# Residual, carried norms and scaled copies: one block per slot, and no POOL weight block in the attention output and the first feed-forward quad

## The chip, the cores and the metric

One NeuronCore of a Trainium2 chip runs the whole program. The metric is the time of one execution on the device in microseconds, lower is better. Engines have short names here: PE (TensorE, matmul), PEld (its weight loads), DVE (VectorE), ACT (ScalarE), POOL (GpSimd), SP (SyncE, which issues the DMAs). Each engine works through its own instructions in a fixed order; an instruction that waits holds up those behind it on the same engine.

## The reference

A decoder layer for 256 prompt tokens and 8 sample tokens, D_MODEL 2048, in fp32:

```python
def decoder_layer(x, mem_k, mem_v, st, p):
    y, st_new = token_mixers(x, st, p)          # four branches, gated, merged, @ w_out
    x = layer_norm(DN_ALPHA * x + y, p["ln1_g"], p["ln1_b"])
    x = layer_norm(DN_ALPHA * x + memory_attention(x, mem_k, mem_v, p), p["ln2_g"], p["ln2_b"])
    x = layer_norm(DN_ALPHA * x + sq_relu_mlp(x, p), p["ln3_g"], p["ln3_b"])
    return x, st_new

def layer_norm(x, g, b):
    mu = jnp.mean(x, axis=-1, keepdims=True)
    var = jnp.mean(jnp.square(x - mu), axis=-1, keepdims=True)
    return (x - mu) * lax.rsqrt(var + LN_EPS) * g + b

def memory_attention(x, mem_k, mem_v, p):       # 4 heads of 128, 256 memory tokens
    q = x @ p["xq_w"]
    a = softmax(q . mem_k * XDH ** -0.5)
    return (a . mem_v) @ p["xo_w"]

def sq_relu_mlp(x, p):                          # 2048 -> 8192 -> 2048
    h = jnp.square(jax.nn.relu(x @ p["ffn_w1"] + p["ffn_b1"]))
    return h @ p["ffn_w2"] + p["ffn_b2"]
```

The token mixers (a delta rule, two convolutions, an mLSTM) come first and take the first half of the time; the change does not touch them.

## The kernel before

**Layout.** Activations are kept transposed: 128 features by 264 tokens is one block, and a row of 2048 features is 16 blocks (`KB`). `y` holds the residual stream, one block per `d`.

**Precision.** Every large product is made of three matmuls in fp32r: an operand is split into a high part (rounded) and a low part (the rest), and high × high, high × low and low × high are summed in PSUM. For weights, `wh` and `wl` are made on the chip: ACT rounds `raw` into `wh` (`feed`), and DVE or POOL subtracts to get `wl` (`feed_lo`). For activations the pairs are `xh`/`xl`, `zh`/`zl`, `hgh`/`hgl`, `mh`/`ml`.

**Slots.** The program is one long list of slots. A slot is a weight block of 128 × 1024 and its 24 matmuls. While slot s runs on PE, `run` (L287) issues `wh` and `wl` of slot s + 2 and the load of slot s + 5 (`dma_w`; three `raw` buffers). Every `every[0]`-th block has its `wl` made on POOL (`slot`, L206): every fourth at first, every third from the query projection on (L1448), every second from the first feed-forward layer on (L1667).

**Work between slots.** Work that no slot owns is written as Python generators, which `run` steps once or more a slot: `chain` (one step when DVE is not behind by its own estimate `dv_t`) and `fill` (as many steps as that estimate leaves room for). What is issued then goes through a scheduler, which orders the instructions of each engine by a simulated timeline; `after(i, "DVE")` ties an instruction behind the last `wl` of DVE, and nothing else holds a generator's work to the slot in which it was issued. The generators that matter here:
- `residual` (L1307) writes ALPHA·x, less a rough mean `m`, into `y` from the pair `xh`, `xl`, during the last branch's projection.
- `Norm` (L377) gathers the sums of y and y² block by block (`add`: the squares on ACT, the even blocks' sums on POOL, the odd ones' on DVE) and makes mean and 1/σ from them (`finish`).
- `carry` (L1361) rewrites `y` for the next residual: (y − mean)·(ALPHA·g)·(1/σ) + ALPHA·b for 16 blocks, with every second subtraction on POOL (`Norm.block`) and the shift `ab` on ACT.

**The norm inside a product.** The product after a norm does not wait for the norm. It multiplies by y·g (`z_block`, L1331: `zh` on ACT, `zl` on DVE), with two more columns for the sums over g and b (`zpair`), and the mean and 1/σ are put in when PSUM is read (`z_post`, L1337).

**Stages around the change**, in slots: the last branch's projection with its gates (`stage2`, L1373); output projection `wout`, 32; query projection, 8, in a quad (four PSUM banks at once); memory keys, 8; memory values, 8, with the attention (`attn`) as a chain beside both; attention output `xo`, 8 (L1626, two banks `gxo` a slot); the first quad of the first feed-forward layer, 8; the rest of the hidden group (24 slots); then output and hidden groups by turns, to the final norm. PE has four PSUM banks for products (`pg`, L95).

## Time and profile before

| | |
|---|---|
| median of 3 runs | 2326.68 us (2324.32 to 2328.25) |
| the profiled execution | 2324.7 us, span 2322.9 us |
| PE busy | 2249.0 us, 97% of the span |
| DVE, ACT, POOL busy | 1269.8, 1167.0, 977.8 us |
| mean granted clock of PE | 0.990 |

A busy time is a sum over the whole span. Where PE is idle, and at which clock it runs after it, is read from windows of some stages; 1.00 there is the higher of two levels of the clock, 2.4 GHz, and 0.50 the lower one, 1.2 GHz. A duration in the trace overlaps with that of the next instruction on the same engine; what an instruction costs in a queue is the distance between two starts.

### The profile page before, as it was taken

Reading aid. Unit: us, or ns where it says so; the run is one execution under the profiler, and the core shown is the slowest. Engines: PE = TensorE matmul, PEld = TensorE weight load, DVE = VectorE, ACT = ScalarE, POOL = GpSimd, SP = SyncE. Lnnn points to the kernel's source line nnn. Section 1 sums busy time; section 2 is a strip of 40 time slices with the busy share of each in tenths; the row PEclk is TensorE's granted clock in tenths of the full one; section 3 lists DMA queues with packets and bytes.
Section 4 is the critical chain, followed back from the end, with each engine's and each line's share of the span. In section 5 each row is a group of like instructions: output and inputs, shape, how many; then the busy total and the mean of one; then the engine's idle time right before and its main releaser. Section 6 shows DMA issues by size and latency. Waiting matters only on the chain.

```text
span 2322.9 us, 46442 instructions
## 1 busy us (share of the span) xinstructions
PE 2249.0 (97%) x19034; PEld 2205.4 (95%) x19034; DVE 1269.8 (55%) x2039; ACT 1167.0 (50%) x1789; POOL 977.8 (42%) x733
## 2 busy tenths in 40 slices
PE   9899999989999999999989999989999999999997
PEld 8899898989999999999989998889999999999997
DVE  7998998894464455433474566385323323323323
ACT  6756456554554455544434555456435435534543
POOL 4535335341222133433243365165445544544576
PEclk9999999999999999999999999999999999999998
DMA  7556455554656676765556666545565565566553
GB/s 233 166 151 201 137 174 167 169 165 143 193 173 185 195 221 215 211 182 182 182 183 182 200 200 201 187 132 181 181 182 176 179 182 181 174 183 181 176 180 127
DMA packets 125134, 418.81 MB, mean 180 GB/s; under 512 B 15608, under 2 KB 20984, under 8 KB 124920
## 3 DMA queue, kind: packets, MB, share of 16 engines
q1 hardware_dynamic: 124920, 415.84, 58.4%
q8 instruction: 149, 2.44, 0.4%
q14 instruction: 65, 0.53, 0.1%
HBM read 401.37 MB, written 14.41 MB: 179 GB/s over the span
## 4 chain that ended last, share of the span: by engine, by line
PE 81%; DVE 13%; issue 3%; DMA 1%; ACT 1%; POOL 1%; DVEq 0%; POOLq 0%; ACTq 0%; SPq 0%
PE g L150 73%; DVE cB L139 3%; DVE wl L128 3%; PE q L150 1%; DVE cu L139 1%; DVE y L128 1%; PE pv L150 1%; DVE y L139 1%; DMA dbc<-dd 1%; PE ub L150 0%; PE xb L150 0%; DVE s L139 0%; PE cb L150 0%; ACT wh L123 0%; PE nb L150 0%
## 5 line engine op out<-in xcount | busy, mean ns | idle before, releaser
L123 ACT ACTIVATE wh<-raw 128x1024 fp32r<-128x1024 f32 (+1 forms) x705 | 745.4, 1058 | 822.4 <-PE g L150 306.3
L128 POOL TENSOR_TENSOR wl<-raw,wh 128x1024 fp32r<-128x1024 f32 x240 | 588.0, 2450 | 724.7 <-PE g L150 483.2
L150 PE MATMUL g<-xh,wl 128*128 128x264 f32 x2496 | 714.0, 286 | 8.1 <-DVE wl L128 6.0
L150 PE MATMUL g<-xl,wh 128*128 128x264 f32 x2496 | 717.2, 287 | 0.0
L150 PE MATMUL g<-xh,wh 128*128 128x264 f32 x2496 | 716.1, 287 | 0.9 <-ACT wh L123 0.9
L128 DVE TENSOR_TENSOR wl<-raw,wh 128x1024 fp32r<-128x1024 f32 (+1 forms) x465 | 589.8, 1269 | 231.2 <-PE g L150 169.6
L150 PEld LDWEIGHTS g<-xh,wl 128*128 128x128 f32 x2496 | 473.0, 190 | 10.2 <-DVE wl L128 6.6
L150 PEld LDWEIGHTS g<-xh,wh 128*128 128x128 f32 x2496 | 473.5, 190 | 5.3 <-issue 2.5
L150 PEld LDWEIGHTS g<-xl,wh 128*128 128x128 f32 x2496 | 472.2, 189 | 2.3 <-issue 1.3
L150 PE MATMUL g<-hgh,wl 128*128 128x264 f32 x1024 | 290.4, 284 | 0.0
L150 PE MATMUL g<-hgl,wh 128*128 128x264 f32 x1024 | 290.4, 284 | 0.0
L150 PE MATMUL g<-hgh,wh 128*128 128x264 f32 x1024 | 289.9, 284 | 0.0
L150 PE MATMUL g<-zh,wh 128*128 128x266 f32 x960 | 275.1, 287 | 0.8 <-DVE zw L128 0.8
L150 PE MATMUL g<-zl,wh 128*128 128x266 f32 x960 | 274.6, 286 | 0.0
L150 PE MATMUL g<-zh,wl 128*128 128x266 f32 x960 | 274.4, 286 | 0.0
L150 PEld LDWEIGHTS g<-hgl,wh 128*128 128x128 f32 x1024 | 193.0, 188 | 0.0
L150 PEld LDWEIGHTS g<-hgh,wh 128*128 128x128 f32 x1024 | 192.5, 188 | 0.0
L150 PEld LDWEIGHTS g<-hgh,wl 128*128 128x128 f32 x1024 | 192.4, 188 | 0.0
L128 DVE TENSOR_TENSOR y<-y,g 128x264 f32<-128x264 f32 x80 | 34.3, 429 | 278.7 <-PE g L150 278.7
L150 PEld LDWEIGHTS g<-zh,wh 128*128 128x128 f32 x960 | 181.4, 189 | 1.0 <-ACT wh L123 1.0
L150 PEld LDWEIGHTS g<-zl,wh 128*128 128x128 f32 x960 | 181.7, 189 | 0.0
L150 PEld LDWEIGHTS g<-zh,wl 128*128 128x128 f32 x960 | 180.8, 188 | 0.0
(481 smaller groups left out, 3449.3 us busy)
## 6 DMA issues: line engine op xcount, KB each, us to landing
raw<-in_win_dram SPq DMA_DIRECT2D x312, 512.0 KB, 4.0
raw<-in_f_dram SPq DMA_DIRECT2D x248, 512.0 KB, 4.2
raw<-in_wbr_dram SPq DMA_DIRECT2D x64, 512.0 KB, 4.0
raw<-in_wout_dram SPq DMA_DIRECT2D x32, 512.0 KB, 4.3
s<-in_sS_dram SPq DMA_DIRECT2D x8, 512.0 KB, 5.0
dbc<-dd SPq DMA_DIRECT2D x16, 256.0 KB, 3.7
out_S_s_dram<-s SPq DMA_DIRECT2D x8, 512.0 KB, 5.2
c<-in_sCm_dram SPq DMA_DIRECT2D x8, 512.0 KB, 5.7
```

Of the source, the lines that this page charges most:

```text
L123: return AC.activation(out, in_, func, bias=bias, scale=scale, **kw)
L128: return (eng or DV).tensor_tensor(out=out, in0=a, in1=b, op=op)
L139: return DV.scalar_tensor_tensor(out=out, in0=a, scalar=s, in1=b, op0=op0, op1=op1)
L150: PE.matmul(out, lhsT, rhs, start=start, stop=stop)
```

## The change

Five edits.
- A third queue, `pace`: `run` steps it exactly once a slot, before the others and without a look at the estimate. The residual, both `carry` generators and the new `z_two` go through it.
- In `residual` each block is two instructions on DVE (the subtraction of `m` goes into the first of them, and none is on POOL), tied behind the last `wl`, with a `yield` after each block.
- In `carry` both instructions of a block run on DVE and are tied behind the last `wl`; ACT's addition of the shift is gone, and the shift is added with the attention output and with the first output group of the feed-forward layer, in one instruction with the addition of the product.
- `z_block` scales on ACT into a buffer `zf`, rounds that on ACT into `zh`, and subtracts on DVE. After the attention output it no longer stands in the slot's `post` but in `z_two`, one block a slot until all products are there and two a slot then, tied behind the last `wl`; the carried norm follows in the same generator.
- `every[0] = 0` from the attention output on: no `wl` on POOL there and in the first quad of the feed-forward layer, until `every[0] = 2`.

```diff
     def slot(src, fn, post=None):
         seen[0] += 1
-        on_pool = len(slots) > 8 and seen[0] % every[0] == 0
+        on_pool = len(slots) > 8 and every[0] and seen[0] % every[0] == 0
...
                 feed_lo(s + 2)
+            if pace:
+                step(pace)
             if chain and dv_t[0] < lim:
...
-        def block(self, d, gcol, pool=False):
+        def block(self, d, gcol, pool=False, held=False):
             t = self.y[:, d, :]
-            tt(t, t, self.mu, SUB, eng=GP if pool else None)
-            stt(t, t, gcol, self.rs, MUL, MUL)
+            x = tt(t, t, self.mu, SUB, eng=GP if pool else None)
+            y = stt(t, t, gcol, self.rs, MUL, MUL)
+            if held:
+                after(x, "DVE")
+                after(y, "DVE")
...
         for d in range(KB):
             t = y[:, d, :]
-            ts(t, al[:, d, :].bitcast(F32), ALPHA, MUL)
-            if d:
-                tt(t, t, m[:], SUB, eng=GP if d % 2 else None)
-            stt(t, ah[:, d, :].bitcast(F32), ALPHA, t, MUL, ADD)
+            if d == 0:
+                after(ts(t, al[:, d, :].bitcast(F32), ALPHA, MUL), "DVE")
+            else:
+                after(stt(t, al[:, d, :].bitcast(F32), ALPHA, m[:], MUL, SUB), "DVE")
+            after(stt(t, ah[:, d, :].bitcast(F32), ALPHA, t, MUL, ADD), "DVE")
+            yield
...
-    def z_block(n, d):
+    def z_block(n, d, held=False):
         zh, zl = yt["z" + n]
         g, y = col(yt["zg"], d), yt["y"][:, d, :]
-        act(zh[:, d, 0:NT], y, AF.Copy, scale=g)
-        stt(zl[:, d, 0:NT], y, g, zh[:, d, 0:NT].bitcast(F32), MUL, SUB)
+        z = tp.tile([P, 30 + NT], F32, tag="extB", name="zf")[:, 0:NT]
+        act(z, y, AF.Copy, scale=g)
+        act(zh[:, d, 0:NT], z, AF.Copy)
+        x = tt(zl[:, d, 0:NT], z, zh[:, d, 0:NT].bitcast(F32), SUB)
+        if held:
+            after(x, "DVE")
...
         for d in range(KB):
-            t = ln.block(d, yt["ag"][:, i, d:d + 1], pool=d % 2)
-            act(t, t, AF.Identity, bias=yt["ab"][:, i, d:d + 1])
-            if d % 2:
-                yield
+            ln.block(d, yt["ag"][:, i, d:d + 1], held=True)
+            yield
...
+    def z_two(ln):
+        for d in range(KB):
+            while yt["ny"] <= d:
+                yield
+            z_block("2", d, held=True)
+            ln.add(d)
+            if yt["ny"] < KB or d % 2 or d == KB - 1:
+                yield
+        yield from carry(1, ln)
...
     mark(xo_start)
+    every[0] = 0
...
                 t = yt["y"][:, d, :]
-                tt(t, t, yt["pxo"][i], ADD)
-                z_block("2", d)
-                yt["ln"].add(d)
+                stt(t, yt["pxo"][i], yt["ab"][:, 0, d:d + 1], t, ADD, ADD)
+            yt["ny"] += 2
...
-                tt(t, t, ps, ADD)
+                if g:
+                    tt(t, t, ps, ADD)
+                else:
+                    stt(t, ps, yt["ab"][:, 1, d:d + 1], t, ADD, ADD)
```

How the instructions of DVE stand before and after, at three places. A row names the line, the operation, what it writes and reads, the shape and, where it repeats, how often.

The residual on DVE, before (`y<-xl` and `y<-xh,y` make a block, `m` is the rough mean, `wl` a weight block's low part, `gate` and `ml` the branch's own work):

```order
L133 TENSOR_SCALAR y<-xl 128x264 x11
L133 TENSOR_SCALAR gb<-pc 128x16
L143 COPY gb<-pc 128x16
L128 TENSOR_TENSOR wl<-raw,wh 128x1024
L128 TENSOR_TENSOR ab<-ab,bm 128x32
L128 TENSOR_TENSOR y<-y,m_14309 128x264 x8
L128 TENSOR_TENSOR gate<-g,gate 128x264
L139 SCALAR_TENSOR_TENSOR y<-xh,y 128x264
L128 TENSOR_TENSOR wl<-raw,wh 128x1024
L139 SCALAR_TENSOR_TENSOR y<-xh,y 128x264 x12
L128 TENSOR_TENSOR wl<-raw,wh 128x1024
```

The same place after:

```order
L128 TENSOR_TENSOR wl<-raw,wh 128x1024
L128 TENSOR_TENSOR ab<-ab,bm 128x32
L128 TENSOR_TENSOR y<-y,m_14340 128x264
L138 SCALAR_TENSOR_TENSOR y<-xl,m_14340 128x264
L138 SCALAR_TENSOR_TENSOR y<-xh,y 128x264
L128 TENSOR_TENSOR gate<-g,gate 128x264
L128 TENSOR_TENSOR wl<-raw,wh 128x1024
L138 SCALAR_TENSOR_TENSOR y<-xl,m_14340 128x264
L128 TENSOR_TENSOR ml<-merged,mh 128x264
L138 SCALAR_TENSOR_TENSOR y<-xh,y 128x264
L128 TENSOR_TENSOR wl<-raw,wh 128x1024
```

Twelve blocks stood between two `wl`; now one block does, or two where a block of POOL falls between.

The first carried norm on DVE at the query projection, before (`a` holds the norm's sums, then mean and 1/σ; `q_...` are the quad's banks):

```order
L128 TENSOR_TENSOR y<-y,a_15921 128x264 x5
L139 SCALAR_TENSOR_TENSOR a_15921<-q,a_15920 128x264
L128 TENSOR_TENSOR y<-y,a_15921 128x264 x3
L128 TENSOR_TENSOR wl<-raw,wh 128x1024
L139 SCALAR_TENSOR_TENSOR y<-y,ag,a_15921 128x264 x12
L128 TENSOR_TENSOR wl<-raw,wh 128x1024
L139 SCALAR_TENSOR_TENSOR y<-y,ag,a_15921 128x264 x4
L128 TENSOR_TENSOR wl<-raw,wh 128x1024 x2
L143 COPY zw<-q_17056 128x2
```

The same place after:

```order
L138 SCALAR_TENSOR_TENSOR a_15906<-q,a_15905 128x264
L128 TENSOR_TENSOR wl<-raw,wh 128x1024
L128 TENSOR_TENSOR y<-y,a_15906 128x264
L138 SCALAR_TENSOR_TENSOR y<-y,ag,a_15906 128x264
L128 TENSOR_TENSOR wl<-raw,wh 128x1024
L128 TENSOR_TENSOR y<-y,a_15906 128x264 x2
L138 SCALAR_TENSOR_TENSOR y<-y,ag,a_15906 128x264 x2
L128 TENSOR_TENSOR wl<-raw,wh 128x1024
L128 TENSOR_TENSOR y<-y,a_15906 128x264
L138 SCALAR_TENSOR_TENSOR y<-y,ag,a_15906 128x264
L128 TENSOR_TENSOR wl<-raw,wh 128x1024
```

The pieces of 8, 12 and 4 have become blocks of one or two between the `wl`; POOL's eight subtractions are among them.

The attention output on DVE, before, from the third product on (`gxo` is a product, `zl` the low scaled copy, `a` the odd blocks' norm sums):

```order
L128 TENSOR_TENSOR y<-y,gxo 128x264
L128 TENSOR_TENSOR wl<-raw,wh 128x1024
L139 SCALAR_TENSOR_TENSOR zl_18158<-y,pc,zh_18157 128x264
L128 TENSOR_TENSOR a_18156<-a_18156,ln_z 128x264
L128 TENSOR_TENSOR a_18156<-a_18156,y 128x264
L139 SCALAR_TENSOR_TENSOR zl_18158<-y,pc,zh_18157 128x264
L128 TENSOR_TENSOR y<-y,gxo 128x264 x2
L139 SCALAR_TENSOR_TENSOR zl_18158<-y,pc,zh_18157 128x264
L128 TENSOR_TENSOR a_18156<-a_18156,ln_z 128x264
L128 TENSOR_TENSOR a_18156<-a_18156,y 128x264
L128 TENSOR_TENSOR y<-y,gxo 128x264 x2
L128 TENSOR_TENSOR wl<-raw,wh 128x1024
```

The same place after:

```order
L138 SCALAR_TENSOR_TENSOR y<-gxo,ab,y 128x264
L128 TENSOR_TENSOR wl<-raw,wh 128x1024
L128 TENSOR_TENSOR zl_18159<-zf,zh_18158 128x264
L128 TENSOR_TENSOR a_18157<-a_18157,ln_z 128x264
L128 TENSOR_TENSOR a_18157<-a_18157,y 128x264
L138 SCALAR_TENSOR_TENSOR y<-gxo,ab,y 128x264 x2
L128 TENSOR_TENSOR zl_18159<-zf,zh_18158 128x264
L128 TENSOR_TENSOR wl<-raw,wh 128x1024
L128 TENSOR_TENSOR a_18157<-a_18157,ln_z 128x264
L128 TENSOR_TENSOR zl_18159<-zf,zh_18158 128x264
L128 TENSOR_TENSOR a_18157<-a_18157,y 128x264
L138 SCALAR_TENSOR_TENSOR y<-gxo,ab,y 128x264 x2
```

One `zl` a slot stands there in place of two, and a `wl` in every slot; the norm's sums are not tied and stand as they did.

On SP's queue the four loads of `cv` for the second half of the samples stand one block earlier, ahead of the fourth block of the memory values' weights instead of behind it.

## Rows read from the trace of the kernel before

**Rows 1.** The page, its first line and part 1 (busy, share, instructions).

```profile
span 2322.9 us, 46442 instructions
PE 2249.0 (97%) x19034; PEld 2205.4 (95%) x19034; DVE 1269.8 (55%) x2039; ACT 1167.0 (50%) x1789; POOL 977.8 (42%) x733
```

**Rows 2.** Waits of PE, 1100 to 1700 us: total, times, longest.

```profile
PE q L150 <- DVE wl L128: 8.1, 3, 4.1
...
PE gxo L150 <- DVE y L128: 3.1, 1, 3.1
```

**Rows 3.** Windows: width, busy time (instructions) of PE, PEld, DVE, ACT, POOL, clock, DMA.

```profile
1180.00:1200.00 20.00, 12.10 (x76) 11.25 (x75) 17.78 (x28) 5.91 (x8) 12.56 (x9) 0.83 0.44 141
1200.00:1220.00 20.00, 20.00 (x167) 20.00 (x167) 7.99 (x10) 8.73 (x12) 7.18 (x4) 1.00 0.51 159
```

**Rows 4.** Tiles g, q, gxo: ns least/median/most, first and last start.

```profile
L150 PE MATMUL g<-hgh,wl x1024: 279/283/292, 1646.8 to 2304.2; 128*128 128x264 f32 x171
L150 PE MATMUL g<-zh,wh x960: 280/286/361, 1575.2 to 2210.4; 128*128 128x266 f32 x192
...
L150 PE MATMUL q<-zh,wh x128: 282/287/480, 1411.8 to 1573.8; 128*128 128x266 f32 x128
L143 DVE COPY zw<-q x4: 149/152/159, 1443.3 to 1448.4; 128x2 f32<-128x2 f32 x4
L128 DVE TENSOR_TENSOR zw<-q,fb x4: 145/155/160, 1574.4 to 1579.7; 128x2 f32<-128x2 f32 x4
...
L150 PE MATMUL gxo<-ox,wh x128: 278/284/557, 1510.4 to 1540.5; 128*128 128x264 f32 x128
```

**Rows 5.** Timeline of DVE at the attention output: start, duration.

```profile
1518.06 0.43 DVE L128 TENSOR_TENSOR y<-y,gxo 128x264 f32<-128x264 f32 x1 [0.19 <-PE gxo L150]
...
1523.61 0.48 DVE L139 SCALAR_TENSOR_TENSOR zl<-y,pc,zh 128x264 fp32r<-128x264 f32 x1
1524.01 0.42 DVE L128 TENSOR_TENSOR y<-y,gxo 128x264 f32<-128x264 f32 x1
1524.35 1.44 DVE L128 TENSOR_TENSOR wl<-raw,wh 128x1024 fp32r<-128x1024 f32 x1
1525.72 0.98 DVE L139 SCALAR_TENSOR_TENSOR zl<-y,pc,zh 128x264 fp32r<-128x264 f32 x1
1526.62 2.59 DVE L128 TENSOR_TENSOR a<-a,ln_z 128x264 f32<-128x264 f32 x1
...
1551.37 1.22 DVE L128 TENSOR_TENSOR wl<-raw,wh 128x1024 fp32r<-128x1024 f32 x1
1552.51 0.42 DVE L128 TENSOR_TENSOR a<-a,a 128x264 f32<-128x264 f32 x1
```

**Rows 6.** Timeline of DVE at the residual and the first carried norm.

```profile
1184.13 9.13 DVE L139 SCALAR_TENSOR_TENSOR y<-xh,y 128x264 f32<-128x264 f32 x12
...
1426.51 7.05 DVE L139 SCALAR_TENSOR_TENSOR y<-y,ag,a 128x264 f32<-128x264 f32 x12
```

**Rows 7.** The page, part 6 (issues: KB each, us to landing).

```profile
raw<-in_win_dram SPq DMA_DIRECT2D x312, 512.0 KB, 4.0
```

**Rows 8.** Timeline of POOL at the attention output.

```profile
1526.37 2.54 POOL L128 TENSOR_TENSOR wl<-raw,wh 128x1024 fp32r<-128x1024 f32 x1
```

**Rows 9.** POOL by line and shape, 1510 to 1576 us.

```profile
L128 POOL TENSOR_TENSOR a<-a,ln_z 128x264 f32<-128x264 f32 x7 | 7.6, 1091 | 1.7 <-ACT ln_z L123 1.6
```

**Rows 10.** Window of the output projection, columns as in rows 3.

```profile
1330.00:1411.00 81.00, 81.00 (x673) 81.00 (x672) 50.79 (x54) 42.70 (x62) 53.16 (x36) 1.00 0.63 199
```

**Rows 11.** POOL by line and shape, 1580 to 1650 us.

```profile
L128 POOL TENSOR_TENSOR wl<-raw,wh 128x1024 fp32r<-128x1024 f32 x13 | 31.3, 2405 | 4.3 <-ACT wh L123 1.9 <-ACT relu L123 1.8 <-PE g L150 0.5
L128 POOL TENSOR_TENSOR relu<-relu,a 128x264 f32<-128x264 f32 x14 | 11.3, 804 | 26.7 <-DVE relu L139 25.1 <-DVE zw L128 1.6
```

**Rows 12.** DVE and ACT by line and shape, 1320 to 1410 us.

```profile
L139 DVE SCALAR_TENSOR_TENSOR zl<-y,pc,zh 128x264 fp32r<-128x264 f32 x15 | 11.3, 753 | 5.4 <-ACT zh L123 5.2
...
L123 ACT ACTIVATE wh<-raw 128x1024 fp32r<-128x1024 f32 x32 | 33.9, 1058 | 34.7 <-DMA raw<-in_wout_dram 27.8 <-PE g L150 5.3 <-DMA raw<-in_xq_dram 1.5
```

More of the change, by code (lines that the diff above doesn't have):

```diff
@@ L132, in ts @@
         if op1 is None:
-            DV.tensor_scalar(out, a, s1, None, op0=op0)
-        else:
-            DV.tensor_scalar(out, a, s1, s2, op0=op0, op1=op1)
+            return DV.tensor_scalar(out, a, s1, None, op0=op0)
+        return DV.tensor_scalar(out, a, s1, s2, op0=op0, op1=op1)
     def stt(out, a, s, b, op0, op1):
@@ L201, in decoder_step @@
     slots, fed, hl = [], [0], {}
-    chain, fill = deque(), deque()
+    chain, fill, pace = deque(), deque(), deque()
     marks = {}
@@ L223, in drain @@
     def drain(g):
-        for q in (chain, fill):
+        for q in (chain, fill, pace):
             while g in q:
@@ L1317, in residual @@
                 yield
-                tt(t, t, m[:], SUB)
-            if d % 2:
-                yield
+                after(tt(t, t, m[:], SUB), "DVE")
     def zpair(n, g, b):
@@ L1364, in carry @@
         for d in range(KB):
-            t = ln.block(d, yt["ag"][:, i, d:d + 1], pool=d % 2)
-            act(t, t, AF.Identity, bias=yt["ab"][:, i, d:d + 1])
-            if d % 2:
-                yield
+            ln.block(d, yt["ag"][:, i, d:d + 1], held=True)
+            yield
     s2 = ExitStack()
@@ L1387, in stage2 @@
         gens["r1"] = residual(yt["y"], xh, xl)
-        fill.append(gens["r1"])
+        pace.append(gens["r1"])
         for i in range(4):
@@ L1430, in after_wout @@
         gens["c1"] = carry(0, yt["ln"])
-        chain.append(gens["c1"])
+        pace.append(gens["c1"])
         att = yt["yp"].tile([P, KB * NT], F32, tag="y16", name="att")
@@ L1623, in xo_start @@
         zpair("2", "l2g", "l2b")
+        yt["ny"] = 0
+        gens["c2"] = z_two(yt["ln"])
+        pace.append(gens["c2"])
+    def z_two(ln):
[7 more added lines that the diff above has]
+        yield from carry(1, ln)
     mark(xo_start)
+    every[0] = 0
     for dd_ in range(8):
@@ L1645, in after_xo @@
         s2.close()
-        gens["c2"] = carry(1, yt["ln"])
-        chain.append(gens["c2"])
     mark(after_xo)
```

## The prediction

> **What bounds the kernel now.** I read the page first: TensorE (PE) is busy for 97% of the span [rows 1], so nothing can be won but PE's idle time and the half-clock stretches behind it. The waits of PE between 1100 and 1700 us come next: nearly all name VectorE (DVE), by the low part of a weight block (wl) or by a y that frees a PSUM bank [rows 2]. Then the windows of 20 us, to size what is lost in a stage whose matmuls are all alike: 76 matmul records from 1180 to 1200 us against 167 in the next window, at a mean clock of 0.83 [rows 3]. So (167 − 76) / 167 × 20 = 10.9 us are lost at the residual, waiting and half-clock matmuls together.
>
> The tile views give the slot: from the first hidden-layer matmul (1575.2) to the last one of the output layer (2304.2) PE runs 248 slots without a wait, 2.94 us each [rows 4]. With that the two other places are sized. The query stage has 8 slots, 23.5 us; it runs from 1411.8 to its first column copy at 1443.3, 31.5 us [rows 4]. Its sums of the norm take some 0.4 (an estimate: four short matmuls), so 7.6 us are lost. The attention output and the first quad of the feed-forward stage are 16 slots, 47.0 us; they take from 1510.4 to 1574.4, 64.0 us [rows 4]. Of the rest, 1.8 stays in both kernels: the av matmuls and their split lie between the first two slots, and the third y there comes at 1518.06, 7.7 after the first gxo, where two slots are 5.9 [rows 4, 5]. With 0.3 for the norm's sums the stage could be 49.1: 14.9 us are lost.
>
> **Residual.** Before, DVE runs 12 adds in one piece from 1184.13 for 9.13 us, with the next wl behind them [rows 6]; PE stands for it. The change issues two DVE instructions per slot behind that slot's wl, and no POOL one. Each lasts about 0.42 and lets the next start after 0.34, with a column as scalar after 0.40 [rows 5]: 0.8 at most in a slot, beside one wl of 1.14 [rows 5] and the gate work. In a stage where DVE is busy 7.99 of 20 us [rows 3], that adds 5.4 per 20: no queue. Behind each held instruction stands the next slot's wl, which has two slots of lead. The one latency is the first block: the mean (DVE, PE, ScalarE, DVE) with the next wl behind it. I keep 0.4 for it and count 10.5 saved (bounds 9 to 10.9).
>
> **First carried norm.** Before, 12 multiplications in one piece take DVE 7.05 us from 1426.51, with wl blocks queued behind [rows 6]. After, one block a slot: one subtraction and one multiplication, 0.34 + 0.40 = 0.74 on DVE. Two blocks fall between two wl where a third block goes to POOL, 2.6 us for two slots with the wl: nothing stalls. The 16 additions on ScalarE go; the shift comes in with the attention output's addition. I count 7.3 of 7.6 (bounds 5.5 to 7.6). On the SP queue the four cv loads now stand ahead of the fourth value block instead of behind it. A load of 512 KB lands in 4.0 us [rows 7]; if four of them delay that block by 4 to 8 us, it still has some four slots, 11.8 us, before its matmuls: nothing.
>
> **Attention output and first quad.** This is where the change gives less than is lost. In steady state a slot now puts on DVE: one wl 1.14, two y additions with a column (0.40 each), one scaled low copy 0.34 (a plain subtraction; 0.40 before), two norm sums 0.68. That is 2.96 us, against 2.94 of PE. Before, it was two thirds of a wl and two low copies: 0.76 + 0.68 + 0.80 + 0.68 = 2.92, no less. The gain is on POOL: its weight blocks here lasted 2.54 us, and a norm sum of DVE that met one lasted 2.59 instead of 0.42 [rows 5, 8]; a wl beside POOL's sums lasted 1.44 against 1.22 alone [rows 5]. What stays on POOL are two norm sums in a slot, 1.09 us each [rows 9]. One of them makes a low copy 0.98 instead of 0.48 [rows 5]: 0.5 each, so a slot costs DVE 3.96 us. Six slots (the third to the eighth) run late by 6 × 1.02 = 6.1; PE has four banks, two per slot, so it can be one slot (2.9) ahead before it waits: 3.2 us late at the quad. There a slot is one wl and two low copies, 1.82, and DVE catches up. With 0.5 for the quad's last two banks the stage is 49.1 + 3.2 + 0.5 = 52.8, and 11.2 us are saved. Bounds: 14.9 if POOL's sums cost DVE nothing; with each sum added whole a slot is 2.96 + 2.18 = 5.14, PE is 6 × 2.20 − 2.9 = 10.3 late and 4.1 is saved. I take 0.5 since it is the excess of the nearest row.
>
> The y addition is read from PSUM, and such additions last 0.42 or 0.43 beside POOL's work as without it [rows 5]. The Trainium skill (SBUF — State Buffer, section "SBUF: two separate sides") says that a DVE instruction with two SBUF inputs and a POOL instruction lock each other out for a whole instruction. The trace agrees at the norm sum: POOL's weight block runs from 1526.37 to 1528.91, the sum from 1526.62 to 1529.21 [rows 5, 8]. By that rule of the Trainium skill a slot's instructions other than the y additions exclude POOL's sums, 2.16 + 2.18 = 4.34 us, and 8.9 instead of 11.2 would be saved.
>
> The second pass on ScalarE (scale, then round) is 0.41 longer per block, an estimate from DVE's 0.42 for the same tile; ScalarE is busy 42.70 of 81 us at the output projection [rows 10], so it has room. In the last stages 48 additions take a column, 0.06 more each, beside a slot of 2.94 of which DVE needs little: nothing.
>
> **First hidden group.** The second carried norm moves on into it, 15 blocks. Two slots there hold 1.14 + 2 × 0.74 on DVE and about 0.9 of hidden-block work, 3.5 of 5.9; POOL has a wl of 2.41 and a sum of 0.80 [rows 11]. Added whole they are 6.7, 0.8 too much: 6.6 in eight pairs, less the lead of one to two slots (2.9 to 5.9). I keep 0.3 (bounds 0 to 3.7).
>
> **Sum.** 10.5 + 7.3 + 11.2 − 0.3 = 28.7 us. The profiled execution took 2324.7, of which the span is 2322.9 [rows 1]; the run lies 2.0 below the median of 2326.68. From the profiled one 2296.0 follows, from the median 2298.0, which I predict.
>
> **Rivals.**
> - *The pacing hides all.* POOL's few sums miss DVE's instructions; 10.9 + 7.6 + 14.9 = 33.4, 2293. For it: DVE's own 2.96 is just a slot. Against it: the 0.98 of the low copy [rows 5]. 0.2.
> - *Locked out.* Each sum of POOL adds its whole length to DVE: 4.1 at the attention output and −3.7 in the hidden group, 10.5 + 7.3 + 4.1 − 3.7 = 18.2, 2308. For it: the 2.59 [rows 5]; against it: the low copy that grew by 0.5 only. By the rule of the Trainium skill named above, which spares the y additions, it would be 2300 with the hidden group at 0.3. 0.15.
> - *Slower: the low copies hold DVE.* In DVE's order each stands ahead of a wl, in the output projection too, and it now waits for two ScalarE passes. Per block of two slots DVE there has 50.79 / 81 × 5.88 = 3.7 us of work, 2.2 free [rows 10]; today all low copies wait 5.2 us for ScalarE [rows 12]. From 2.2 us a block on PE waits. If ScalarE put two weight blocks (2 × 1.06) and a wait for their load between the passes, some 4.7 us, 16 × 2.5 = 40 us are lost: 2338. For it: ScalarE waits 27.8 us for loads there [rows 12]. Against it: in the order of the change the two passes stand together, ahead of the next weight block. 0.05.
> - *It does not pace.* The scheduler could still bunch the blocks, and the time would stay at 2326. The order shows one or two blocks between wl, so only the norm sums, which are not held, can run ahead. 0.03.
>
> **How the numbers follow.** Forecast 0.57, rivals as above. About 0.2% (4.7 us) is what a measurement tells from no change. Forecast and the first two rivals are all faster by more: 0.92; the unpaced case and a small part of the slower one give 0.03 for the same; slower 0.05. The forecast's own range is 2294 to 2303. The range of 8 in 10 takes in the full gain (2324.3, the lowest run, less 33.4 is 2291) and the locked case: 2290 to 2309.
>
> **What would show it.** Right: 165 or more matmul records in each 20 us at the residual, with clock 1.00; no wait of PE for wl in the query stage, and its first column copy some 24 us after its first matmul; in the attention output waits of PE for y of about 1 us each, together 2 to 4, and no POOL wl until the hidden group; DVE's sums at most about 1 us long. Wrong: a DVE wait for a low copy's ScalarE pass followed by a PE wait for wl; PE waits in the first hidden group; or a stage of 16 slots longer than 58 us.

## The result, and the profile after

The changed kernel takes 2298.3 us (median of 4 runs, 2297.17 to 2300.5), against 2327.34 (2324.32 to 2328.25, 4 runs) for the kernel before beside it: ratio 0.9879, 95% interval 0.9861 to 0.9896, so 29.0 us less. Forecast were 2298.0. The profiled execution took 2300.5 us. Its page, first line and part 1 (against [rows 1]):

```profile
span 2298.7 us, 46421 instructions
PE 2243.9 (98%) x19034; PEld 2202.1 (96%) x19034; DVE 1283.6 (56%) x2054; ACT 1163.0 (51%) x1789; POOL 935.0 (41%) x703
```

The windows at the residual (columns as in [rows 3]):

```profile
1180.00:1200.00 20.00, 20.00 (x168) 20.00 (x167) 15.91 (x20) 8.58 (x11) 7.88 (x4) 1.00 0.70 227
1200.00:1220.00 20.00, 20.00 (x168) 20.00 (x167) 19.04 (x29) 9.78 (x13) 7.60 (x5) 1.00 0.69 201
```

PE does not stop at the residual any more: 168 matmul records in 20 us, against 76 in [rows 3], at a clock of 1.00. The tiles of after, to be set beside [rows 4], and from the same view of both kernels two tiles that rows 4 don't hold, the last matmuls before the change and the last of the projection in which the residual stands (before's lines are those with L150):

```profile
L150 PE MATMUL g<-pairC,wh x256: 278/283/389, 501.7 to 664.5; 128*128 128x264 f32 x128
L150 PE MATMUL g<-xh,wh x2496: 278/283/479, 32.7 to 1315.1; 128*128 128x264 f32 x192
```

```profile
L149 PE MATMUL g<-pairC,wh x256: 278/283/389, 504.1 to 666.8; 128*128 128x264 f32 x128
L149 PE MATMUL g<-xh,wh x2496: 278/283/567, 33.0 to 1306.5; 128*128 128x264 f32 x192
L149 PE MATMUL q<-zh,wh x128: 280/286/480, 1403.0 to 1546.2; 128*128 128x266 f32 x128
L142 DVE COPY zw<-q x4: 151/156/160, 1426.7 to 1433.4; 128x2 f32<-128x2 f32 x4
L149 PE MATMUL gxo<-ox,wh x128: 278/283/471, 1493.5 to 1520.4; 128*128 128x264 f32 x128
L128 DVE TENSOR_TENSOR zw<-q,fb x4: 146/150/152, 1548.4 to 1552.3; 128x2 f32<-128x2 f32 x4
L149 PE MATMUL g<-hgh,wl x1024: 279/283/292, 1622.5 to 2280.0; 128*128 128x264 f32 x171
```

With these starts the program falls into stretches that can be compared from kernel to kernel, whatever went before. The columns: *residual*, from the last pairC to the last xh matmul; *output projection*, from there to the first q; *query*, to the first column copy; *16 slots*, from the first gxo to the first zw of the first quad; *rest*, from there to the last hgh matmul. The stretch between query and attention output is 66.6 to 67.1 us in all kernels. Us, each from these tile rows of its own profile:

| kernel | residual | output projection | query | 16 slots | rest | median |
|---|---|---|---|---|---|---|
| before | 650.6 | 96.7 | 31.5 | 64.0 | 729.8 | 2327.3 |
| after | 639.7 | 96.5 | 23.7 | 54.9 | 731.6 | 2298.3 |
| after, a second time (e9) | 639.5 | 96.1 | 23.7 | 53.6 | 731.7 | 2297.5 |
| residual alone (e1) | 640.0 | 96.1 | 32.5 | 63.9 | 731.4 | 2317.6 |
| first norm in a piece (e7) | 639.7 | 96.1 | 32.4 | 53.6 | 732.4 | 2308.3 |
| POOL blocks kept (e2) | 639.6 | 96.6 | 23.7 | 57.4 | 732.2 | 2302.4 |
| sums on DVE (e3) | 639.7 | 96.1 | 25.3 | 51.7 | 732.0 | 2296.0 |
| carry later (e4) | 639.5 | 96.1 | 23.7 | 52.7 | 732.8 | 2297.5 |
| no POOL blocks in the first group (e5) | 639.8 | 96.1 | 23.7 | 52.5 | 729.8 | 2294.8 |
| low copy from y (e8) | 639.5 | 96.2 | 23.7 | 52.6 | 732.6 | 2297.4 |
| nothing on POOL (e6) | 640.2 | 96.7 | 24.8 | 50.6 | 730.0 | 2294.5 |
| the same, sums paced (e10) | 639.6 | 96.0 | 23.7 | 50.6 | 729.9 | 2294.7 |
| the same, low copy from y (e11) | 639.5 | 96.7 | 23.6 | 49.2 | 731.1 | 2292.4 |

So in after's profile 10.9 us come from the residual, 7.8 from the query stage, 9.1 from the 16 slots, and 1.8 are lost again in the rest. Before the last pairC, where nothing was changed, after's profile is 2.3 us later than before's; over all profiles that start lies between 663.6 and 670.1. That, and 1 to 1.6 us in stages whose code is equal (the query column of e3 and e6), is the spread behind every single profile here. The second part has a visible cause: in the query stage of e3 a sum of the norm on DVE (a<-a,a) began 0.3 us after a POOL weight block and lasted 2.33 us instead of 0.43, in e6 a pair of carried multiplications lasted 3.03 instead of 0.89 beside one. Which instruction meets a POOL block changes from run to run. One run of the kernel with POOL's blocks kept (3087.24 us, against 2302.34 to 2303.04 of its other three) is left out of its median.

What PE still waits for, 1100 to 1700 us (against [rows 2]):

```profile
PE g L149 <- DVE zw L128: 2.5, 1, 2.5
PE gxo L149 <- ACT ln_z L123: 0.6, 1, 0.6
PE q L149 <- DVE y L138: 0.5, 2, 0.3
PE gxo L149 <- DVE y L138: 0.5, 1, 0.5
PE g L149 <- POOL wl L128: 0.2, 1, 0.2
```

The longest is at a place where before waited 0.8 us. DVE's timeline at the end of the quad (start, duration), and POOL's in the same place:

```profile
1542.87 1.22 DVE L128 TENSOR_TENSOR wl<-raw,wh 128x1024 fp32r<-128x1024 f32 x1
1544.00 2.63 DVE L128 TENSOR_TENSOR y<-y,a 128x264 f32<-128x264 f32 x1
1546.56 0.42 DVE L138 SCALAR_TENSOR_TENSOR a<-q,a 128x264 f32<-128x264 f32 x1
1548.02 0.49 DVE L138 SCALAR_TENSOR_TENSOR y<-y,ag,a 128x264 f32<-128x264 f32 x1 [1.04 <-ACT a L123]
1548.43 0.15 DVE L128 TENSOR_TENSOR zw<-q,fb 128x2 f32<-128x2 f32 x1
```

```profile
1543.95 2.40 POOL L128 TENSOR_TENSOR wl<-raw,wh 128x1024 fp32r<-128x1024 f32 x1 [17.49 <-PE q L149]
```

```profile
1540.00:1560.00 20.00, 17.52 (x129) 17.28 (x127) 16.01 (x28) 12.03 (x22) 9.73 (x6) 0.91 0.45 136
1560.00:1580.00 20.00, 20.00 (x164) 20.00 (x163) 18.17 (x29) 10.71 (x18) 11.86 (x7) 1.00 0.50 158
```

POOL's first weight block after the pause starts 0.05 us before the first subtraction of the second carried norm, and that lasts 2.63 us instead of 0.43. Behind it on DVE stand the variance (a<-q,a) and the four outputs of the quad, so the first zw comes 1.7 us after the quad's last matmul (started at 1546.49, 0.28 long). PE stands 2.5 us, and in the window around it (columns as in rows 3) the granted clock is 0.91, part of it at the lower of its two levels (1.2 and 2.4 GHz). At that level the matmuls start 0.22 us apart (1551.79, 1552.01, 1552.23), and from 1553.3 on 0.12 again; 16 of them cost 1.6 us more. That is nearly all of the 1.8 us that the rest loses in this profile: the next window is full, at a clock of 1.00, and up to 1700 us PE waits no more.

### The profile page after: what moved, and what is told of

It is laid out like the page before. It is cut to its first block, busy times and chain, and to the rows that moved or that the text cites. A ratio compares the mean times of both kernels' runs of the same rounds, so it can differ in the third digit from the quotient of the medians.

```text
span 2298.7 us, 46421 instructions
## 1 busy us (share of the span) xinstructions
PE 2243.9 (98%) x19034; PEld 2202.1 (96%) x19034; DVE 1283.6 (56%) x2054; ACT 1163.0 (51%) x1789; POOL 935.0 (41%) x703
## 4 chain that ended last, share of the span: by engine, by line
PE 83%; DVE 11%; DMA 2%; ACT 2%; issue 2%; POOL 1%; SPq 0%; DVEq 0%; POOLq 0%; ACTq 0%
PE g L149 74%; DVE cB L138 3%; DVE wl L128 2%; PE q L149 2%; DVE cu L138 1%; PE pv L149 1%; DMA mr<-in_memT_dram 1%; ACT wh L123 1%; DVE y L128 1%; DMA dbc<-dd 1%; PE ub L149 0%; PE ob L149 0%; PE xb L149 0%; PE cb L149 0%; PE nb L149 0%
## 5 line engine op out<-in xcount | busy, mean ns | idle before, releaser
L128 POOL TENSOR_TENSOR wl<-raw,wh 128x1024 fp32r<-128x1024 f32 x234 | 573.0, 2449 | 712.6 <-PE g L149 489.4
L128 DVE TENSOR_TENSOR hgl<-relu,hgh 128x264 fp32r<-128x264 f32 x64 | 42.2, 664 | 197.9 <-ACT hgh L123 197.9
```

Source lines behind the costliest of these rows:

```text
L128: return (eng or DV).tensor_tensor(out=out, in0=a, in1=b, op=op)
```

## The experiments

Ratios are to the kernel before, run on the same chip; after stands at 0.9879 (0.9861 to 0.9896). In every diff + and - are against the kernel named.

**e1: the residual alone, in the kernel before.**

```diff
+            if pace:
+                step(pace)
...
-        fill.append(gens["r1"])
+        pace.append(gens["r1"])
```

with the new `residual`. 

> The kernel before with the paced residual only (the queue that is stepped once a slot, two held DVE instructions a block, none on POOL). Theory: DVE's piece of 12 additions with the weight block behind it is the whole loss of that place and of no other, so its 10.9 us come back: about 2316. Rival: the three places depend on each other, and what is won here is in part lost at the query stage or the attention output: under 6 us saved, over 2320. The matmul records of the 20 us at the residual should be 165 or more in both.

Measured 2317.59 us (2315.61 to 2318.38), ratio 0.9956 (0.9941 to 0.9970), 9.4 below before. The residual's stretch is 640.0 us, 10.6 less than before and within 0.5 of after's; 167 records in each window of 20 us. The query stage takes 1.0 us more than before (32.5), the 16 slots are as long (63.9). So the three losses are separate ones and can be added. What the median shows less than 10.6 lies in the query stage and in the rest, which takes 1.6 us more (731.4): after the quad PE waits, with the second carried norm as it was, nearly as long as in after:

```profile
PE g L149 <- DVE zw L128: 2.4, 1, 2.4
```

Here 16 carried multiplications stand in one piece ahead of zw on DVE (6.55 us from 1558.63). The granted clock falls after this stop too, to 0.91 in the 20 us from the first zw.

One thing is not separated. The edit spreads the blocks and takes eight subtractions from POOL at once, and in before these ran beside the piece. POOL by line and shape, before, 1165 to 1200 us:

```profile
L128 POOL TENSOR_TENSOR y<-y,m 128x264 f32<-128x264 f32 x8 | 11.8, 1513 | 3.1 <-DVE y L133 3.1
```

The 12 additions took 9.13 us, 0.76 each, where one lets the next start after 0.34 when nothing is in the way [rows 5]. The other half fits POOL's work beside it, the last of these subtractions and a weight block of 2.54 us. That a piece stops PE without such help, the 16 multiplications above show: they ran at 0.41 each, and PE stood 2.4 us. How much the piece at the residual would cost alone, or blocks spread out with POOL's part kept, no run shows.

**e7: the first carried norm in a piece, the rest as in after.**

```diff
-        pace.append(gens["c1"])
+        chain.append(gens["c1"])
...
-            ln.block(d, yt["ag"][:, i, d:d + 1], held=True)
-            yield
+            ln.block(d, yt["ag"][:, i, d:d + 1], pool=not i and d % 2, held=i)
+            if i or d % 2:
+                yield
```

> The kernel after, but the first carried norm is stepped two blocks at a time from the general queue again, with every second subtraction on POOL and none held; its shift stays out of ScalarE. Theory (12 multiplications in one piece on DVE with the weight blocks behind them are the loss of the query stage): DVE runs some 12 multiplications for about 5 to 7 us, PE waits for wl, the query stage takes 31 instead of 23.7 us, 7 to 8 us slower than the kernel after, about 2306. Rival (the loss was shared with the additions on ScalarE, which stay out): under 4 us slower.

Measured 2308.3 us (2306.27 to 2309.4), ratio 0.9917 (0.9902 to 0.9932): 10.0 above after's median, 8.7 in the query stage's own stretch (32.4 against 23.7). DVE's timeline there shows the piece again, and PE waits 5.8 us for wl, as in [rows 2]:

```profile
1408.69 6.77 DVE L128 TENSOR_TENSOR y<-y,a 128x264 f32<-128x264 f32 x8
1415.38 1.76 DVE L128 TENSOR_TENSOR wl<-raw,wh 128x1024 fp32r<-128x1024 f32 x1
1417.06 7.07 DVE L138 SCALAR_TENSOR_TENSOR y<-y,ag,a 128x264 f32<-128x264 f32 x12
```

The additions of the shift on ScalarE were left out here too, and the loss came back whole, so they had cost nothing. What came back is the piece on DVE together with POOL's eight subtractions: DVE's eight took 6.77 us, 0.85 each, while POOL did its own from 1408.80 to 1416.06. As in e1, the two are not separated.

**e2: POOL's weight blocks kept in the 16 slots.**

```diff
-    every[0] = 0
     for dd_ in range(8):
```

> The kernel after, but every third weight block of the attention output and first quad goes to POOL again. Theory (POOL's block of 2.4 to 2.5 us holds up the DVE instruction that it meets, and that costs more than the 1.14 us that DVE is spared): 5 such blocks, each 2.2 of hold-up less 1.14, so 5 to 6 us slower than the kernel after, about 2304, with norm sums or low copies of 2.5 us in DVE's timeline. Rival (the one block per slot is what won the time, and POOL's blocks cost nothing or relieve DVE): within 1.5 us of the kernel after, or faster.

Measured 2302.43 us (2302.34 to 2303.04), ratio 0.9894 (0.9878 to 0.9910): 4.1 above after's median, 2.5 to 3.8 of it in the 16 slots (57.4 against 54.9 and 53.6). POOL makes six weight blocks in that stretch, and four of them show in DVE's timeline as a sum or a low copy that is 1.6 to 2.2 us too long, two of them in pairs with one of 0.4 (the sixth meets the first carried subtraction, 2.62 us, as in after):

```profile
1508.95 2.62 DVE L128 TENSOR_TENSOR a<-a,ln_z 128x264 f32<-128x264 f32 x1
...
1521.53 2.54 DVE L128 TENSOR_TENSOR zl<-zf,zh 128x264 fp32r<-128x264 f32 x1
...
1531.77 2.97 DVE L128 TENSOR_TENSOR zl<-zf,zh 128x264 fp32r<-128x264 f32 x2
...
1542.01 2.39 DVE L128 TENSOR_TENSOR zl<-zf,zh 128x264 fp32r<-128x264 f32 x2 [0.77 <-ACT zh L123]
```

So of the 9 to 10 us won in the 16 slots, some 3 are owed to the pause of POOL's blocks, and the larger part to the other edits there: one block per slot, the shift in the addition, all carried subtractions on DVE. These no run takes apart. The theory was right in sign, its size (5 to 6) a little too large; the rival falls.

**e3: the second norm's even sums on DVE.**

```diff
-            a, e = self.a[i], None if i else GP
+            a, e = self.a[i], None if i or not self.pool else GP
```

> The kernel after, but the second norm's sums of even blocks run on DVE too, so POOL has nothing in the attention output. Theory (a POOL sum makes a DVE instruction 0.5 us longer): a slot of DVE goes from 2.96 + 2 x 0.5 = 3.96 to 2.96 + 0.68 = 3.64, so it ends 6 x 0.32 = 1.9 us less late: 1 to 2 us faster than the kernel after, and all weight blocks there at 1.1 to 1.25, all low copies at 0.43. Rival (POOL's sums cost DVE nothing on the path that counts): 1 to 2 us slower, since DVE has 0.68 more to do. Rival (each POOL sum is added whole, 1.09): 6 us or more faster.

Measured 2296.02 us (2294.8 to 2299.71), ratio 0.9868 (0.9854 to 0.9882), 2.3 below after's median and 1.5 below its second (e9), with intervals that overlap; 16 slots in 51.7 us. DVE by line and shape in the 16 slots (total busy, mean ns), first after, then e3:

```profile
L128 DVE TENSOR_TENSOR wl<-raw,wh 128x1024 fp32r<-128x1024 f32 x15 | 19.5, 1303 | 0.8 <-ACT wh L123 0.8
L128 DVE TENSOR_TENSOR zl<-zf,zh 128x264 fp32r<-128x264 f32 x16 | 8.8, 561 | 3.7 <-ACT zh L123 3.6
L138 DVE SCALAR_TENSOR_TENSOR y<-gxo,ab,y 128x264 f32<-128x264 f32 x16 | 7.5, 482 | 1.1 <-PE gxo L149 1.0
L128 DVE TENSOR_TENSOR a<-a,y 128x264 f32<-128x264 f32 x6 | 3.7, 611 | 0.0
L128 DVE TENSOR_TENSOR a<-a,ln_z 128x264 f32<-128x264 f32 x7 | 3.5, 501 | 0.0
```

```profile
L128 DVE TENSOR_TENSOR wl<-raw,wh 128x1024 fp32r<-128x1024 f32 x15 | 18.3, 1219 | 2.2 <-ACT wh L123 2.2
...
L128 DVE TENSOR_TENSOR zl<-zf,zh 128x264 fp32r<-128x264 f32 x16 | 6.7, 427 | 1.1 <-ACT zh L123 1.1
L128 DVE TENSOR_TENSOR a<-a,ln_z 128x264 f32<-128x264 f32 x14 | 5.9, 427 | 0.0
L128 DVE TENSOR_TENSOR a<-a,y 128x264 f32<-128x264 f32 x12 | 5.0, 427 | 0.0
```

With POOL empty every low copy lasts 0.43 and every weight block 1.22. In after the same instructions, 44 with the sums, are longer by 1.2 + 2.1 + 6 × 0.18 + 7 × 0.07 = 4.9 us. POOL does 14 sums there (28 of them are on DVE in e3, two of a form not shown, and 14 in after), so one of them costs DVE about 0.35 us; doing it on DVE costs 0.34, from one start to the next [rows 5]. So by these durations POOL gave no relief at all. That e3 gains time all the same fits the order: a sum of DVE's own can wait until the quad, where DVE has room, behind the y additions that free PE's banks (12 of the 28 stand there in e3, 3 of the 14 in after), while the lengthening falls on whatever runs beside POOL. From 16 to 32 us after the first gxo (1509.5 to 1525.5 us in after) PE has 110 matmul records, in e3 and e6, without POOL's sums, 133. So sums moved to DVE cost PE nothing there, against the first rival.

**e4: the second carried norm one slot later.**

```diff
         yield from ln.finish()
         yield
+        if i:
+            yield
         for d in range(KB):
```

> The kernel after, with the second carried norm's blocks one slot later, so that none stands ahead of the quad's end. Theory (the first held subtraction meets POOL's first weight block, lasts 2.63 instead of 0.42 and holds up the variance behind it; the four outputs of the quad then come 2 us late, PE waits 2.5 us for zw and runs at half clock after): zw 2 us earlier, PE's wait for it under 0.5, 2.5 to 4 us faster than the kernel after, 2294 to 2296. Rival (the chain variance, 1/sigma, four outputs, and the POOL multiplication behind them sets the wait anyway, or the next two-input instruction meets POOL's block instead): under 1 us.

Measured 2297.51 us (2296.14 to 2298.14), ratio 0.9871 (0.9857 to 0.9885), 0.8 below after: a miss. The step at the quad's end worked: the variance comes right behind its weight block, and the 16 slots take 52.7 us, 2.2 less than in after's first profile and 0.9 less than in its second. But the rest takes 1.1 to 1.2 more (732.8), with three waits of PE for POOL's wl, 1.3 us in all. The blocks now meet the next two POOL weight blocks, as DVE and POOL show:

```profile
1548.91 3.02 DVE L138 SCALAR_TENSOR_TENSOR y<-y,ag,a 128x264 f32<-128x264 f32 x2
...
1554.93 3.53 DVE L128 TENSOR_TENSOR y<-y,a 128x264 f32<-128x264 f32 x2
```

```profile
1549.13 2.52 POOL L128 TENSOR_TENSOR wl<-raw,wh 128x1024 fp32r<-128x1024 f32 x1 [0.91 <-ACT relu L123]
...
1555.58 2.60 POOL L128 TENSOR_TENSOR wl<-raw,wh 128x1024 fp32r<-128x1024 f32 x1
```

And the second run of after (e9, below) shows that its wait of 2.5 us was partly chance.

**e5: no weight block on POOL in the whole first group.**

```diff
-        every[0] = 2
+        every[0] = 2 if g else 0
```

> The kernel after, with no weight block on POOL in the whole first group of hidden blocks and its output layer, not only up to the quad. Theory (the first POOL block lasts 2.40 and holds the first held subtraction for 2.63, the variance behind it comes 2.2 us late, PE waits 2.5 us for zw and then runs at half clock for a while): the four outputs of the quad start within 1 us of its last matmul, no wait of PE for zw or for POOL's wl, 2.5 to 4 us faster than the kernel after, 2294 to 2296. Rival (DVE then has 2 x 1.14 + 2 x 0.74 + about 1.0 = 4.8 us in two slots of 5.88 and meets POOL's 0.8 of multiplication: it is full and falls behind): within 1 us of the kernel after, or slower, with PE waits for DVE's wl in the hidden group.

Measured 2294.77 us (2294.05 to 2296.47), ratio 0.9860 (0.9844 to 0.9877), 3.5 below after and 2.7 below its second (e9); its slowest run lies below the fastest of after's first four. The rest is back at before's 729.8 us, and 16 slots take 52.5. No wait of PE for zw or for POOL's wl is left, only some for y. These are all of its waits from 1290 us to 2300:

```profile
PE gxo L149 <- DVE y L138: 1.1, 2, 0.6
PE q L149 <- DVE y L138: 0.5, 2, 0.3
```

DVE, with 18.87 and 18.37 of 20 us busy there, has just room for it. So the theory holds: what after still loses behind the quad goes with POOL's weight blocks holding up DVE, not with the carried blocks as such. Of the three later kernels without these blocks two have it too (e6 730.0, e10 729.9); e11 has 731.1, so a spread of 1 us remains.

**e8: the low copy from y.**

```diff
-        act(z, y, AF.Copy, scale=g)
-        act(zh[:, d, 0:NT], z, AF.Copy)
-        x = tt(zl[:, d, 0:NT], z, zh[:, d, 0:NT].bitcast(F32), SUB)
+        act(zh[:, d, 0:NT], y, AF.Copy, scale=g)
+        x = stt(zl[:, d, 0:NT], y, g, zh[:, d, 0:NT].bitcast(F32), MUL, SUB)
```

> The kernel after, but each scaled block is made as before: one pass of ScalarE (scale and round at once), and the low copy from y by the DVE instruction that takes the scale as a column. Theory (the second ScalarE pass is hidden, DVE's low copy is 0.06 us longer): within 1 us of the kernel after, 0.5 slower if anything, and the low copies' wait for ScalarE falls from 17.1 us to some 5 without any change in PE's waits. Rival (the two passes delay the low copies, and weight blocks queue behind them): 2 us or more faster.

Measured 2297.41 us (2297.3 to 2301.95), ratio 0.9876 (0.9861 to 0.9891), 0.9 below after: no difference, as expected. From 1300 to 1560 us the low copies wait 6.2 us for ScalarE instead of 17.1, and the time stays: in this kernel the two passes are hidden.

**e6: nothing on POOL.** The edits of e3, e4 and e5 together. 

> The kernel after with three edits together: the second norm's sums all on DVE, its carried blocks one slot later, no weight block on POOL in the first group. Theory (what is left of the loss is DVE held up by POOL): 2.3 us for the sums, and 2.5 to 4 for the quad's end with the hidden group, together 5 to 6 us faster than the kernel after, 2292 to 2293.5; 16 slots in 50 us or less. Rival (DVE becomes the bound of the first hidden group): 2295 or more, with PE waits for DVE there.

Measured 2294.49 us (2292.41 to 2295.07), ratio 0.9857 (0.9842 to 0.9872), 3.8 below after; expected were 5 to 6. The 16 slots do take 50.6 us and the rest 730.0, so 4.3 and 1.6 less than in after's first profile; 3.0 and 1.7 less than in its second. In the profiled run 1.1 us of that is lost again in the query stage (24.8 against 23.7), whose code is the same: it is the pair of 3.03 us named above, beside a POOL block of the first norm's stage. From e5 and e3 its median differs by 0.3 and 1.5 us, with overlapping runs.

**e9, e10, e11: on one chip.** After again, unchanged. 

> The kernel after, unchanged, on the chip of the next two, so that they can be compared with it and the spread between runs of one kernel be seen. All theories: 2297 to 2300, with the stage of 16 slots at 54 to 55 us and PE's wait of some 2.5 us for zw at the quad's end.

2297.5 us (2296.14 to 2300.85), ratio 0.9880 (0.9866 to 0.9895). Its PE waits only 0.6 us for zw, and its 16 slots take 53.6 us, though the program is the same: both were expected otherwise. At the quad's end:

```profile
1541.12 0.43 DVE L128 TENSOR_TENSOR y<-y,a 128x264 f32<-128x264 f32 x1
1541.46 0.42 DVE L138 SCALAR_TENSOR_TENSOR a<-q,a 128x264 f32<-128x264 f32 x1
1542.93 1.95 DVE L138 SCALAR_TENSOR_TENSOR y<-y,ag,a 128x264 f32<-128x264 f32 x1 [1.04 <-ACT a L123]
```

```profile
1542.19 2.40 POOL L128 TENSOR_TENSOR wl<-raw,wh 128x1024 fp32r<-128x1024 f32 x1 [17.50 <-PE q L149]
```

Here DVE was ahead, and the subtraction got through before POOL's block; that held up the next instruction, 1.95 instead of 0.49, behind which nothing urgent stood but zw. Which of the two engines comes first is decided by tenths of a microsecond, and it is worth 1.3 us in the 16 slots. The rest is no shorter for it (731.7): instead of the lower clock after the stop, PE now loses time in the hidden group, with 159 matmul records from 1560 to 1580 us (164 in after) and 153 from 1584.8 to 1604.8, where it stands 0.8 us for a POOL weight block.

In e10 the second norm's squares and sums are tied to the weight block of their slot as well, on top of e6:

```diff
             x = act(z[:], y, AF.Square)
+            if held:
+                after(x, "ACT")
+                after(u, "DVE")
+                after(v, "DVE")
```

> The kernel with nothing on POOL (sums on DVE, carried blocks one slot later, no weight block on POOL in the first group), and besides the second norm's squares and sums held behind the weight block of their slot, so that they spread over 16 slots like the blocks. Theory (in the attention output DVE is then at 1.14 + 0.80 + 0.34 + 0.68 = 2.96 us a slot instead of 3.64, so PE is not late there): 16 slots in 49.5 us instead of 50.6, 0.5 to 1.5 us faster than with nothing on POOL, 2293 to 2294, some 4 to 5 below the kernel after. Rival (the sums now fill the quad's last slots and the variance comes later): 1/sigma late, a PE wait for zw, 1 us or more slower than with nothing on POOL, 2295 or more.

2294.69 us (2292.15 to 2295.85), ratio 0.9863 (0.9846 to 0.9879), 16 slots in 50.6: no gain. From 1520 to 1540 us PE is full (20.00 us busy, 19.80 in e6), but from 1540 to 1560 it is busy 19.20 against 19.76, and DVE's variance there waits 1.0 us for PE's sums, as the rival had it, but not with its loss of 1 us. What one end gave the other took back.

e11 is e6 with the edit of e8. 

> The kernel with nothing on POOL, and the scaled blocks made in one pass of ScalarE with the low copy from y, as before. Theory (the second ScalarE pass is hidden, the low copy 0.06 us longer on a DVE that is full in the attention output): 16 slots in 50.6 to 51.5 us, no more than 1 us from the kernel with nothing on POOL, 2294 to 2295.5. Rival (with POOL empty the two passes of ScalarE are what holds DVE at the quad's end): 1.5 us or more faster, 2293 or less.

2292.38 us (2291.9 to 2293.41), ratio 0.9857 (0.9842 to 0.9872): 5.1 below after on the same chip, with no run in common with after's. That is the rival's time (2293 or less), not the theory's. Its 16 slots take 49.2 us, 0.1 more than what the prediction had worked out as the least. The low copies wait for ScalarE no more (1.7 us in e6, none here), and ScalarE is busy 10.55 of 20 us from 1520 to 1540 against 15.45. But its ratio is that of e6, 0.9857, to the before of each one's own chip, and its interval overlaps with e10's. So the 16 slots are shorter with the single pass, in one profile of each kernel; that it makes the better kernel is not shown.

## Why the prediction was right

- **Residual**, forecast 10.5 of 10.9: right, 10.9 in after and 10.6 alone (e1). The latency kept for the first block was not seen. DVE was held up by POOL there too (15.91 and 19.04 us busy of 20, where 7.99 and 5.4 more were expected; a pair of 0.8 us lasted 2.99 beside a POOL block that began at 1197.47), but two slots of lead covered it. The mechanism is less sure than the size: the working puts the loss down to the piece alone, and POOL's subtractions, beside which it took twice its length, went with it.
- **First carried norm**, forecast 7.3 of 7.6: right, 7.8; 8.7 when it is undone (e7), with the same open point. The query stage now takes 23.7 us, its matmuls and 0.2 more, with no wait of PE for wl.
- **Attention output and first quad**, forecast 11.2 saved, 52.8 us left: 9.1 saved (54.9) in after's first profile, 10.4 (53.6) in its second. So the term was too large by 0.8 to 2.1. Its first part came out: PE was to be 3.2 us late at the quad, and from 16 to 32 us after the first gxo, where e6 has 133 matmul records, after has 110 and e9 105, which is 2.8 and 3.4 us. But the working behind that number did not. A sum on POOL cost DVE 0.35 us, not 0.5; with 0.35 the same working gives 6 × 0.72 − 2.9 = 1.4. And it charges each slot with its two DVE sums, though nothing ties them to the slot: e6, at 3.64 us a slot by that sum, is not late at all. Two errors that cancel are luck. What failed in the total is the step "0.5 for the quad's last two banks": it took the norm to be ready at the last matmul. The variance stands behind a carried block in DVE's order, and that block can meet POOL's first weight block after the pause; the first zw then came 1.7 us after the last matmul. In e5 and e9, without that, the stretch stands at 52.5 and 53.6.
- **First hidden group**, forecast −0.3: it was −1.8 and −1.9 in the two profiles of after. The working itself gave 0.7 to 3.7 (6.6 less 5.9 to 2.9); the 0.3 that was kept lies below that, without a reason. And the two profiles lose it in two ways. In the first, 1.6 of the 1.8 us are the matmuls at the lower clock after the stop at the quad's end, a term that the prediction did not have behind this stage; the stop comes in e1 too, and the rest there is 731.4. In the second it is what the working meant, DVE and POOL sharing 6.7 us in 5.9: one POOL block beside two carried instructions makes 3.0 or 3.5 us of them (e4's rows), the outputs of the hidden blocks queue behind, and PE waits for POOL's next weight block. e5 takes the blocks from POOL and has 729.8 us again.
- **The signs.** As forecast: the windows of the residual, 23.7 us from the first q to the column copy, waits of PE in the attention output and at the quad's start, 1.6 us in all (0.6 of it put down to ACT's ln_z) where 2 to 4 were named, none of them as long as 1 us, no sum of DVE over 0.99 us there, 16 slots below 58. Of those that were to mean wrong one came: PE waits at the start of the hidden group (2.5 us for zw).
- **The sum** of 28.7 came out at 24.2 between the two profiled runs and at 29.0 between the medians. The profile after started 2.3 us late before any changed line, which explains 2.3 of the difference of 4.5; the terms in their own stretches give 10.9 + 7.8 + 9.1 − 1.8 + 0.2 (output projection) + 0.3 (the stretch before the attention output) = 26.5. The close hit of the total is in part luck: gains of 0.9 more than forecast, and losses of 3.6 more, and a spread of about 2.
- **The rivals.** That pacing hides all (2293) was not so; e11, with POOL empty and the single pass, comes to 2292.4, e6 with POOL empty alone to 2294.5. In the 16 slots (54.9 or 53.6 in after, 50.6 in e6, 49.2 in e11) POOL's work was most of what kept it away. Locked out (2308) fell: e3 gained 2.3, not 6. A DVE instruction of 0.42 us that met a POOL block of 2.40 lasted 2.63, 2.62 and 2.54 us (after, e2). The rule of the Trainium skill (SBUF — State Buffer, section "SBUF: two separate sides"), by which a DVE instruction with two SBUF inputs and a POOL instruction that reads SBUF exclude each other for the whole of an instruction, agrees with these rows. For the sums the trace shows less than the rule would take, 0.35 for one of 0.75 to 0.95; some of them met y additions, others waited themselves (POOL's longest is 1.74). That the low copies hold DVE fell: they waited for ScalarE 13.1 us between 1320 and 1412 us, 11 times, and PE waited 0.2 us in the whole output projection. That it does not pace fell with the windows of the residual.

## What to carry to other kernels

Where an engine feeds another by a queue in fixed order, work that has no date of its own belongs into it in pieces no longer than one slot's slack, tied to the slot; a long piece stops the fed engine for most of its length (PE waited 5.8 us behind the pieces of 6.77 and 7.07 us in e7), and the same work spread out, and taken from POOL, cost nothing here. Before giving work to POOL, see what DVE does in the meantime: a POOL instruction that costs DVE as much as it saves (0.35 against 0.34 us a sum here) is no relief, and it moves the loss to whatever stands behind on DVE. And when POOL or a held instruction is let in again after a pause, look at what waits right there: here that was the longest wait left, and tenths of a microsecond decided whether it came.

## What was not expected of the hardware

A POOL instruction of 128 × 1024 (2.40 us) made a DVE instruction on two SBUF tiles 2.63 us long that began 0.05 us later, so it ran for 0.28 us after POOL's end; one that found POOL at work for 0.74 us lasted 1.95. In both cases DVE ended 0.28 to 0.29 us after POOL. Additions that read PSUM (y<-gxo,ab,y) kept 0.48 us, beside POOL's work or not. And the same program took 53.6 or 54.9 us for the same 16 slots, mostly by which of two engines was first at one place.
